# Buffers of five tags handed out by urgency, and two more prices in the plan of a hybrid decoder step

## The chip, the core and the metric

The kernel runs on one NeuronCore of a Trainium2 chip. The metric is the device time of one execution in microseconds (us), the median of several runs. Engines are named as the profile names them: PE is TensorE's matmul, PEld its weight load, DVE VectorE, ACT ScalarE, POOL GpSimd, SP SyncE, which issues most DMAs.

## What is computed

One inference step of a two-layer decoder trunk with width 1024, for a prompt of 2048 tokens and for a group of eight samples with one new token each and 2048 cached positions in pages of 128. Layer 0 joins a chunked spatial gate (A) and stick-breaking attention over eight heads (B); layer 1 joins sparse attention over the 256 best keys of an indexer (C) and causal pooling over windows of 2 to 16 (D). Everything is float32.

```python
hp, kvp, _ = even_mixer(xp, None, w_in_even[j], a_w_sp[j], a_b_sp[j])
past = gather_pages(cache_b_kv[j], page_table)
hs, kvs, vs = even_mixer(xs, past, w_in_even[j], a_w_sp[j], a_b_sp[j])
...
log_keep = jnp.where(mask, jax.nn.log_sigmoid(-z), 0.0)                    # B
later = lax.cumsum(log_keep, axis=3, reverse=True) - log_keep
att = jnp.where(mask, jnp.exp(jax.nn.log_sigmoid(z) + later), 0.0)
...
_, sel = lax.top_k(index, topk)                                            # C
logits = jnp.einsum('bqgrd,bqkgd->bqgrk', qg, k_sel) * HEAD_DIM ** -0.5
p = jax.nn.softmax(logits, axis=-1)
...
xp = post_norm(xp, hp, w_out[layer], ln_g[layer], ln_b[layer])
xs = post_norm(xs, hs, w_out[layer], ln_g[layer], ln_b[layer])
```

## The kernel before

The prompt is worked in four blocks of 512 tokens. A matmul that needs full accuracy is made of three: both operands are split into a high and a low part (`split`, line 640; `load_w`, line 656, for weights). `p0` is the input projection of layer 0, `p1a` and `p1b` are that of layer 1 (lines 735 to 737), `out_proj` is the output projection (lines 1132 to 1134), `mixer_b` is B (`z`, line 1027, then transposes `ps_p`, line 1064), `c_tile` is C (`z_c`, line 1763, read by DVE at line 1765; transposes `ps_pc`, line 1794), `index` and `topk` choose the keys (`z_i`, line 1453). At the end of `topk` DVE loads a flag (line 1594) and jumps over a rare exact search (line 1595); this happens 14 times. `sample0` and `sample1` do the eight samples; `sample1` fetches pages of the C cache with 64 indirect DMAs on POOL's queue (`rows`, line 2244), into two buffers.

`Body` emits all of it once, in a program order in which `par` mixes the streams by estimated costs. Then `Order` makes the order that the engines follow. `gather` collects dependences and, for each tag of tiles, the tiles in program order; `settle` prices every instruction, lets `plan` make 15 orders, replays each under two drawings of slightly changed prices (`replay`), and keeps the order with the least sum; `keep` writes it down as a fixed order for each engine. `plan` is a list scheduler: it starts, on each free engine, the ready instruction with the least rank, and the rank is the latest start that `latest` finds by scheduling backwards from the end.

A tag is a ring of buffers that tiles of one kind share. `plan` hands a tag's buffers out in program order: the next tile of a tag gets one only when the tile ahead of it has been begun. The tags that matter here are three pairs of PSUM banks, `pp` (projections), `pt` (transposes) and `pz` (the logits `z`, `z_c`, `z_i`, and the small `ps_s` and `ps_m`), and two SBUF tags with four buffers each, `tmp` and `ot`. `tmp` holds among others `lng` and `lnb`, the scales and shifts of the layer norm (`ln`, lines 1210 and 1211), in halves of 512 columns.

The plan's prices that the change touches: a DMA lands `DMA_START` (700 ns) + bytes over a rate + `DMA_END` (1500 ns) after its turn; a matmul that follows a pause costs `RESTART` (105 ns) more. The flag load is priced at 1300 ns and the jump at 400 ns.

Of the kernel before, what the change touches and what calls it, by code (L numbers as in the profile page):

```python
# [83 lines left out]


class Order:
# [55 lines left out]
    def gather(self):  # L142
# [174 lines left out]

    def settle(self):

        N, eng = len(self.ins), self.eng  # L320
        self.costs = [self.cost(n) for n in range(N)]
        for g, ms in self.group.items():
            busy = sum(self.costs[m][0] for m in ms)
            self.costs[g] = busy, busy + 170
        self.dma = [e is not None and "DMA" in i.opcode for e, i in zip(eng, self.ins)]
        self.kinds = [self.kind(n) for n in range(N)]
        self.ports = [self.port(n) for n in range(N)]
        self.succ = [[] for _ in range(N)]
        for n, d in enumerate(self.dep):
            for m in d:  # L330
                self.succ[m].append(n)
        self.links()
        draws, mid, best = [self.draw(k) for k in range(self.DRAWS)], self.costs, None
        sem = self.SEM
        for by, near in self.GUESSES:
            self.costs = [(b * by, l * by) if e in self.TAIL else (b, l) for e, (b, l) in zip(eng, mid)]
            self.SEM = near
            self.plan(list(range(N)))
            for _ in range(self.ROUNDS):
                self.SEM = near  # L340
                self.plan(self.latest())
                self.SEM = sem
                x = sum(self.replay(c) for c in draws)
                if best is None or x < best[0]:
                    best = x, self.order, self.after
        self.costs, (_, self.order, self.after) = mid, best

# [15 lines left out]
    def replay(self, cost):  # L363
# [9 lines left out]
        for n in range(N):  # L373
# [4 lines left out]
            left[n] = len(preds[n]) + (n in seq)  # L378
        start, done, idle, dma_end, count = [0.0] * N, [0.0] * N, [0.0] * N, 0.0, 0

# [14 lines left out]
        while ready:  # L395
            s, n = pop(ready)
            if self.ports[n]:
                asked.setdefault(n, s)
                if hold[self.OTHER[eng[n]]] > s:
                    push(ready, (hold[self.OTHER[eng[n]]], n))  # L400
                    continue
            count += 1
            if eng[n] is not None:
                busy, lat = cost[n]
                if self.ports[n]:
                    hold[eng[n]] = s + max(40, busy - self.RELEASE[eng[n]])
                if eng[n] == "PE" and n in seq and self.kinds[n] != self.kinds[seq[n]]:
                    s += 150 if "h" in (self.kinds[n], self.kinds[seq[n]]) else 0
                elif eng[n] == "PE" and n in seq and s > idle[seq[n]] + 1:
                    busy, lat = busy + self.RESTART, lat + self.RESTART  # L410
                start[n], idle[n], done[n] = s, s + busy, s + lat
                if self.dma[n]:
                    dma_end = max(s + self.DMA_START, dma_end) + lat
                    done[n] = dma_end + self.DMA_END
            else:
                start[n] = done[n] = idle[n] = s
            for m in succ[n]:
                left[m] -= 1
                if not left[m]:
                    push(ready, (when(m), m))  # L420
# [4 lines left out]
    def turns(self):  # L425
# [12 lines left out]
        return out  # L438

    def plan(self, rank):  # L440

# [9 lines left out]
        queue = {g: ts[::-1] for g, ts in self.tags.items()}  # L451
        free = {g: max(self.tiles[t].tag_meta.bufs for t in ts) for g, ts in self.tags.items()}
        open_ = dict.fromkeys(queue, True)
        users = {t: len(u) for t, u in self.uses.items()}
        self.after, gone = {}, {g: [] for g in queue}
        since, done, self.begun = [0.0] * N, [0.0] * N, [0.0] * N
# [26 lines left out]
        while count < N:  # L483
            while back and back[0][0] <= now:
                _, g, x = pop(back)
                free[g] += 1
                gone[g].append(x)
                take(g, now)
# [9 lines left out]
            for e, q in ready.items():  # L498
                while q and idle[e] <= now:
# [31 lines left out]
                    if self.dma[n]:  # L531
                        dma_end = max(s + self.DMA_START, dma_end) + lat
                        done[n] = dma_end + self.DMA_END
                    else:
# [7 lines left out]
                    for t in tiles[n]:  # L542
                        g, u = home[t], self.uses[t]
                        if n == u[0]:
                            open_[g] = True
                            for m in u[1:]:
# [12 lines left out]
    def latest(self):  # L559

        N, eng, push, pop = len(self.ins), self.eng, heapq.heappush, heapq.heappop
        cost = self.costs
        lat = [c[1] + self.SEM + (self.DMA_START + self.DMA_END if d else 0) for c, d in zip(cost, self.dma)]
        pred, left = [[] for _ in range(N)], [0] * N
# [48 lines left out]

    def keep(self):
        info = mybir.DependencyInfo(mybir.DependencyClass.NoSync, mybir.DependencyReason.DATA)
# [9 lines left out]
class Body:  # L625
    def __init__(self, ctx, tc, I, O):
        self.ctx, self.tc, self.nc, self.I, self.O = ctx, tc, tc.nc, I, O
        pool = lambda n, b, **k: ctx.enter_context(tc.tile_pool(name=n, bufs=b, **k))
        self.cst = pool("cst", 1)
# [37 lines left out]
    def rsqrt(self, out, var, eps, n):  # L667
# [9 lines left out]
        for _ in range(3):  # L677
# [3 lines left out]
            v.tensor_tensor(out, out, t[:n], op=OP.mult)  # L681

    def ps(self, name, shape=(P, TB)):

        b = next(b for b in BANKS.get(name, "pt").split() if b in self.banks)
        return self.banks[b].tile(list(shape), F32, tag=b, name=name)

    def tmp(self, name):
        return self.loc.tile([P, TB], F32, tag="tmp", name=name, bufs=self.bufs["tmp"])

# [396 lines left out]
    def otile(self, name):  # L1087
        return self.loc.tile([P, TB], F32, tag="ot", name=name, bufs=self.bufs["ot"])

# [1374 lines left out]

def build(nc, shapes):
    I = {n: nc.dram_tensor(n, s, d, kind="ExternalInput").ap() for n, s, d in shapes}
    O = {n: nc.dram_tensor("out_" + n, s, F32, kind="ExternalOutput").ap() for n, s in _OUTS}
    with tile.TileContext(nc, schedule_with_timeline_sim=True) as tc:
        with ExitStack() as ctx:
            body = Body(ctx, tc, I, O)  # L2470
            body.run()
        order = Order(tc, body.lags)
        order.gather()
        order.settle()
        order.keep()

# [12 lines left out]
```

## Time and profile before

| | |
|---|---|
| median of 3 runs | 2790.44 us (2785.44 to 2792.58) |
| the profiled execution | 2784.49 us |
| its span, first to last instruction | 2782.8 us |
| PE busy | 2672.8 us, 96% of the span |
| DVE, ACT, POOL busy | 2060.9, 1604.3, 766.3 us |
| mean granted clock of TensorE | 0.983 |

A busy share says how long an engine had an instruction in work, not that it worked at its best. Idle time of PE is listed with what ended it: the instruction of another engine, or the DMA, whose signal came last. The granted clock is 1.00 at 2.4 GHz and 0.50 at 1.2 GHz.

### The profile page before, as it was taken

To read this page: it belongs to the slowest core of one execution; us is meant where nothing else is said; L and a number is where in the kernel's file an instruction comes from. 1 tells how busy PE (TensorE), PEld (TensorE's weight loads), DVE (VectorE), ACT (ScalarE), POOL (GpSimd) and SP (SyncE) were. 2 spreads that over 40 slices of the span, in tenths; PEclk is the share of its full clock that TensorE was granted. 3 is DMA by queue.
4 is the path that set the end of the run, shared out by engine and by line. 5 is a ranking of instruction groups with operands and counts; after the bars stand their busy time and mean duration, and the time that the engine had idled before them with its cause. 6 is when DMAs were issued, how large, how long until landed. Compare 5 with 4: busy or idle time off the path is not lost. (4 is left out here: it accounts for less than half of the span.)

```text
span 2782.8 us, 52464 instructions
## 1 busy us (share of the span) xinstructions
PE 2672.8 (96%) x17490; PEld 2154.5 (77%) x17490; DVE 2060.9 (74%) x5557; ACT 1604.3 (58%) x3216; POOL 766.3 (28%) x1040
## 2 busy tenths in 40 slices
PE   9999999999999999989899999999999999899996
PEld 7888787777777887768677677778777889898985
DVE  3466568775857886747988888897898788888865
ACT  3434333444444354435657677786686788688854
POOL 0111112210202321033433522334411445344222
PEclk9999999999999999999999999999999999999998
DMA  8666857895777777563764545433675666767462
GB/s 251 168 186 207 266 169 245 242 302 161 224 213 205 222 207 249 181 178 116 211 199 132 166 131 157 127 102 115 190 220 149 199 192 200 221 200 235 125 197 81
DMA packets 538914, 524.58 MB, mean 189 GB/s; under 512 B 43447, under 2 KB 411224, under 8 KB 538607
## 3 DMA queue, kind: packets, MB, share of 16 engines
q1 hardware_dynamic: 528759, 485.34, 58.9%
q0 software_dynamic: 9856, 35.66, 4.1%
q8 instruction: 139, 2.28, 0.3%
q14 instruction: 160, 1.31, 0.1%
HBM read 431.33 MB, written 89.73 MB: 187 GB/s over the span
## 5 line engine op out<-in xcount | busy, mean ns | idle before, releaser
L735 PE MATMUL pp<-xh,wh 128*128 128x512 f32 (+1 forms) x1536 | 624.0, 408 | 2.5 <-ACT wh L661 1.6
L736 PE MATMUL pp<-xl,wh 128*128 128x512 f32 (+1 forms) x1536 | 615.4, 401 | 0.0
L737 PE MATMUL pp<-xh,wl 128*128 128x512 f32 (+1 forms) x1536 | 613.6, 400 | 0.0
L664 DVE TENSOR_TENSOR wl<-wr,wh 128x512 fp32r<-128x512 f32 x520 | 354.5, 699 | 161.7 <-ACT wh L661 146.8
L661 ACT CAST wh<-wr 128x1024 fp32r<-128x1024 f32 x260 | 270.2, 1040 | 321.4 <-PE pp L736 160.2
L735 PEld LDWEIGHTS pp<-xh,wh 128*128 128x128 f32 (+1 forms) x1536 | 287.6, 188 | 67.4 <-issue 8.5
L737 PEld LDWEIGHTS pp<-xh,wl 128*128 128x128 f32 (+1 forms) x1536 | 287.6, 187 | 61.5 <-issue 4.4
L736 PEld LDWEIGHTS pp<-xl,wh 128*128 128x128 f32 (+1 forms) x1536 | 288.2, 188 | 53.9 <-issue 5.3
L1132 PE MATMUL pp_o<-wh,oh 128*128 128x256 f32 x1008 | 294.2, 294 | 5.4 <-DVE xres L1137 3.6
L1133 PE MATMUL pp_o<-wl,oh 128*128 128x256 f32 x1008 | 290.5, 289 | 0.2 <-DVE wl L664 0.2
L1134 PE MATMUL pp_o<-wh,ol 128*128 128x256 f32 x1008 | 288.5, 289 | 0.0
L1065 ACT COPY P<-ps_p 128x512 f32<-128x512 f32 (+2 forms) x320 | 166.5, 524 | 178.3 <-PE ps_p L1064 156.2
L1041 DVE TENSOR_TENSOR_SCAN P<-P,bfst 128x512 f32<-128x512 f32 x192 | 250.0, 1317 | 14.5 <-ACT P L1034 7.6
L1763 PE MATMUL z_c<-ksc,qc 128*128 128x512 f32 (+3 forms) x816 | 221.3, 356 | 22.9 <-DVE mx L1765 13.1
L1781 ACT ACTIVATE zt<-zt,nmax 128x512 f32<-128x512 f32 (+3 forms) x320 | 209.6, 657 | 54.1 <-DVE nmax L1769 52.2
L1750 POOL TENSOR_TENSOR nm<-nm,mk 128x256 f32<-128x256 f32 (+1 forms) x128 | 98.4, 770 | 420.2 <-DMA nm<-bft 161.3
L1796 ACT COPY zt<-ps_pc 128x512 f32<-128x512 f32 (+3 forms) x320 | 163.8, 522 | 81.6 <-PE ps_pc L1794 79.2
L1027 PE MATMUL z<-ks,q 128*128 128x512 f32 (+3 forms) x640 | 195.0, 390 | 13.1 <-DVE mx L1765 5.1
L1132 PEld LDWEIGHTS pp_o<-wh,oh 128*128 128x128 f32 x1008 | 193.3, 192 | 12.6 <-DVE xres L1137 4.6
L1133 PEld LDWEIGHTS pp_o<-wl,oh 128*128 128x128 f32 x1008 | 194.3, 193 | 4.1 <-issue 1.1
L1134 PEld LDWEIGHTS pp_o<-wh,ol 128*128 128x128 f32 x1008 | 193.4, 193 | 4.5 <-issue 2.2
L1509 ACT ACTIVATE mk<-ix,tk_tn 128x1152 int8<-128x1152 f32 (+13 forms) x140 | 183.8, 1313 | 17.7 <-DVE tk_tn L1559 6.6
(455 smaller groups left out, 5518.0 us busy)
## 6 DMA issues: line engine op xcount, KB each, us to landing
pg<-cache_b_kv SPq DMA_DIRECT2D x256, 256.0 KB
wr<-w_in_even SPq DMA_DIRECT2D x112, 512.0 KB
wr<-w_in_odd SPq DMA_DIRECT2D x76, 512.0 KB
wr<-w_out SPq DMA_DIRECT2D x68, 512.0 KB
ks<-ksc SPq DMA_DIRECT2D x80, 256.0 KB
ksc<-kcs SPq DMA_DIRECT2D x80, 256.0 KB
q<-qsc SPq DMA_DIRECT2D x64, 256.0 KB
qc<-qcs SPq DMA_DIRECT2D x128, 128.0 KB
```

The source lines that it names most:

```text
L661: nc.scalar.copy(hi, raw)
L664: e.tensor_tensor(lo[:, c], raw[:, c], hi[:, c].bitcast(F32), op=OP.subtract)
L735: nc.tensor.matmul(ps[:m], wh[:, kt, :m], xh[kt], start=a, stop=False)
L736: nc.tensor.matmul(ps[:m], wh[:, kt, :m], xl[kt], start=False, stop=False)
L737: nc.tensor.matmul(ps[:m], wl[:, kt, :m], xh[kt], start=False, stop=b)
L1027: nc.tensor.matmul(z[:, :n], q2[:, c, t * P:(t + 1) * P].bitcast(F32R), ks[:, :n].bitcast(F32R), start=c == 0, stop=c == 1)
L1041: nc.vector.tensor_tensor_scan(r, r, r, initial=ini, op0=OP.mult, op1=OP.bypass)
L1132: nc.tensor.matmul(ps[:, :256], oh[:, tt], wh[:, k], start=a, stop=False)
L1133: nc.tensor.matmul(ps[:, :256], oh[:, tt], wl[:, k], start=False, stop=False)
L1134: nc.tensor.matmul(ps[:, :256], ol[:, tt], wh[:, k], start=False, stop=b)
L1763: nc.tensor.matmul(z[:, :n], q2[:, c, jj % 2, :].bitcast(F32R), kk, start=c == 0, stop=c == 1)
L1781: nc.scalar.activation(zt, zt, AF.Exp, bias=nmx, accum_out=st["rs"][:, h, c:c + 1])
```

## The change

Two things change in `Order`. First, for five tags (`ot`, `tmp`, `pt`, `pz`, `pp`) `plan` no longer hands buffers out in program order alone. When a buffer is free, `choose` looks at the eight tiles of the tag with the least rank; it takes the first of them for which a free buffer exists whose last tile stands earlier in the program, and for which `safe` finds that all tiles passed over can still be placed. To make the buffer binding, the kernel is built twice: the first build plans and stops with the exception `Planned`; the second gives every tile of these tags the buffer of the plan, as a tag of its own with one buffer (`turn`), and follows the planned order. Of the other tags the plan now notes a buffer as well, but doesn't bind it.

Second, prices: a DMA on POOL's queue (all page gathers) lands 2500 ns later in the plan (`GATHER`), in `plan`, `replay` and `latest`; and in `replay`, by which the 15 orders are compared, a PE instruction that starts over 1300 ns after the one before it (`PAUSE`) opens 4500 ns (`WARM`) in which PE's instructions cost up to twice their time. `plan` itself doesn't know this second price. No instruction of the computation is added or removed.

```diff
+FREELY = ('ot', 'tmp', 'pt', 'pz', 'pp')
...
+    GATHER = 2500
+    PAUSE, WARM = 1300, 4500
+    AHEAD, WINDOW = 10**6, 8
...
+        last = lambda n: max(self.group.get(n, (n,)))
+        self.span = {t: (u[0], max(map(last, u))) for t, u in self.uses.items()}
+        self.free = {g for g, ts in self.tags.items() if g.split("_")[0] in FREELY}
...
+        self.ends = [self.DMA_END + (self.GATHER if e == "POOL" else 0) for e in eng]
...
+                if eng[n] == "PE" and n in seq:
+                    cold = s + self.WARM if s > idle[seq[n]] + self.PAUSE else cold
+                    if s < cold:
+                        busy, lat = busy + min(busy, cold - s), lat + min(busy, cold - s)
...
-                    done[n] = dma_end + self.DMA_END
+                    done[n] = dma_end + self.ends[n]
...
+    def safe(self, queue, held, x, b):
+
+        held = [(f, self.span[t][1] if t else -1) for f, t in held]
+        if x:
+            held[b] = self.span[x]
+        far = max(f for f, _ in held)
+        for t in queue:
+            if t == x:
+                continue
+            first, end = self.span[t]
+            if first > far:
+                return True
+            fit = [(f, k) for k, (f, e) in enumerate(held) if f < first and e < first]
+            if not fit:
+                return False
+            held[max(fit)[1]] = first, end
+        return True
+
+    def choose(self, queue, urgent, free, held, pending, any_):
+
+        least = queue[0]
+        if pending and (not any_ or self.span[pending][0] < self.span[least][0]):
+            return None
+        for x in urgent[:self.WINDOW] if any_ and not pending else ():
+            first = self.span[x][0]
+            if x != least and first > self.span[least][0] + self.AHEAD:
+                continue
+            for _, b in sorted(((held[b][0], b) for b in free if held[b][0] < first), reverse=True):
+                if self.safe(queue, held, x, b):
+                    return x, b
...
-            while queue[g] and free[g] and open_[g]:
-                x = queue[g].pop()
-                if gone[g]:
-                    self.after[x] = gone[g].pop(0)
-                free[g] -= 1
-                open_[g] = False
+            while queue[g] and free[g]:
+                x = self.choose(queue[g], urgent[g], free[g], held[g], open_[g], g in self.free)
+                if x is None:
+                    return
+                x, b = x
...
+    def turn(self, pool, shape, tag, name, **k):
+
+        if tag not in self.made:
+            return pool.tile(shape, F32, tag=tag, name=name, **k)
+        if self.slots:
+            k, tag = {"bufs": 1}, f"{tag}{self.slots[tag][len(self.made[tag])]}"
+        t = pool.tile(shape, F32, tag=tag, name=name, **k)
+        self.made[tag.rstrip("0123456789")].append(t.tensor.name)
+        return t
...
+    try:
+        build(bacc.Bacc("TRN2", target_bir_lowering=False, num_devices=1), shapes)
+    except Planned as x:
+        build(nc, shapes, x.args)
```

## Rows read from the trace of the kernel before

**Rows 1.** The page's head and its part 1: busy time of each engine, share of the span, and instructions.

```profile
span 2782.8 us, 52464 instructions
PE 2672.8 (96%) x17490; PEld 2154.5 (77%) x17490; DVE 2060.9 (74%) x5557; ACT 1604.3 (58%) x3216; POOL 766.3 (28%) x1040
```

**Rows 2.** The view by stretches, over the whole span: start and end, length, then busy time of each engine with its instructions, the granted clock of TensorE, the busy share of the DMA engines and GB/s. The last stretch begins where the last matmul ends.

```profile
0.00:1235.00 1235.00, 1218.04 (x6818) 954.06 (x6819) 808.53 (x1483) 523.01 (x966) 210.22 (x332) 1.00 0.71 215
1235.00:2000.00 765.00, 721.98 (x4788) 560.62 (x4787) 632.40 (x1998) 511.01 (x1125) 281.74 (x415) 0.98 0.54 151
2000.00:2400.00 400.00, 386.92 (x2855) 328.98 (x2854) 336.63 (x1144) 303.72 (x593) 144.78 (x162) 0.99 0.65 195
2400.00:2600.00 200.00, 190.98 (x1622) 174.79 (x1622) 163.88 (x560) 156.60 (x306) 80.12 (x88) 0.96 0.65 202
2600.00:2757.50 157.50, 154.85 (x1418) 136.10 (x1414) 106.65 (x342) 106.93 (x226) 39.77 (x38) 1.00 0.42 132
2757.50:2782.80 25.30, 0.00 (x0) 0.00 (x0) 12.81 (x34) 3.04 (x4) 9.63 (x8) 0.60 0.51 167
```

**Rows 3.** The view of groups by line for PE: line, operation, out<-in, shapes, count, busy us, mean ns of one, then idle time of PE just before them and what ended it.

```profile
L1132 PE MATMUL pp_o<-wh,oh 128*128 128x256 f32 x1008 | 294.2, 294 | 5.4 <-DVE xres L1137 3.6 <-ACT oh L648 0.9 <-DVE fq L1586 0.6
...
L1763 PE MATMUL z_c<-ksc,qc 128*128 128x512 f32 (+3 forms) x816 | 221.3, 356 | 22.9 <-DVE mx L1765 13.1 <-ACT r L1456 2.7 <-DVE s_rq L2124 2.0
L1027 PE MATMUL z<-ks,q 128*128 128x512 f32 (+3 forms) x640 | 195.0, 390 | 13.1 <-DVE mx L1765 5.1 <-DMA ks<-ksc 4.4 <-ACT P L1031 2.2
L1794 PE MATMUL ps_pc<-idf,zt 128*128 128x128 f32 x1088 | 182.0, 279 | 2.0 <-ACT zt L1796 0.7 <-ACT P L1065 0.7 <-ACT s16o L1148 0.4
L1064 PE MATMUL ps_p<-idf,P 128*128 128x128 f32 x1088 | 180.7, 276 | 5.8 <-ACT P L1065 4.6 <-DVE hT L762 1.0
...
L1453 PE MATMUL z_i<-kid,qi 128*128 128x512 f32 (+3 forms) x160 | 63.8, 417 | 7.8 <-DMA qi<-qis 5.4 <-ACT r L1456 1.4 <-DVE mx L1765 0.9
```

**Rows 4.** DVE's first instruction after one of the 14 jumps, in order of time: start us, us, what; in brackets the idle time before it and what ended it.

```profile
1557.80 1.01 DVE L1511 TENSOR_SCALAR_CACHE_REDUCE mk<-ix,tk_tn 128x768 int8<-128x768 f32 x1 [3.63 <-DVEq L1595]
```

**Rows 5.** The view of waits for DVE, two of the nine lines that end on the jump's sequencer: who waited, for what, us in total, times, longest; and the jump's own line.

```profile
DVE mk L1511 <- DVEq L1595: 10.8, 3, 4.1
...
DVE ri L1822 <- DVEq L1595: 0.9, 1, 0.9
```

```profile
L1595 DVEq COMPARE_BRANCH  x14: 56/72/76, 1419.1 to 2643.9; - x14
```

**Rows 6.** PE in order of time: the first, the longest and the last of nine pauses (0.60 to 5.11 us, 20.5 us together) that begin while DVE stands at a jump, or within 6 us after it.

```profile
1495.87 0.58 PE L1763 MATMUL z_c<-ksc,qc 128*128 128x256 f32 x2 [2.05 <-DVE mx L1765]
```

```profile
1562.49 1.01 PE L1027 MATMUL z<-ks,q 128*128 128x384 f32 x2 [5.11 <-DVE mx L1765]
```

```profile
2651.73 0.72 PE L1763 MATMUL z_c<-ksc,qc 128*128 128x512 f32 x2 [1.22 <-DVE mx L1765]
```

**Rows 7.** The view by stretches, over the stretches inside the work in which the granted clock was 0.50, columns as in rows 2: four after jumps, then three after gathers, then two after other waits for PSUM, then three in other places, and their sum.

```profile
1496.20:1499.50 3.30, 3.30 (x10) 2.60 (x9) 3.30 (x9) 1.08 (x3) 1.83 (x2) 0.50 1.06 267
1561.10:1567.80 6.70, 5.31 (x26) 4.57 (x27) 4.47 (x20) 1.69 (x5) 1.96 (x3) 0.50 0.09 23
1643.00:1646.30 3.30, 3.30 (x9) 2.30 (x8) 2.60 (x10) 2.02 (x6) 1.24 (x3) 0.50 0.28 60
2120.80:2124.20 3.40, 3.40 (x11) 2.52 (x10) 3.37 (x10) 3.22 (x4) 0.75 (x2) 0.50 0.00 0
2486.10:2489.40 3.30, 3.30 (x16) 3.11 (x14) 2.83 (x4) 3.30 (x6) 0.67 (x1) 0.50 0.94 311
2516.80:2523.50 6.70, 6.59 (x33) 5.09 (x31) 4.85 (x12) 4.45 (x12) 5.38 (x5) 0.50 0.79 254
2533.90:2540.60 6.70, 6.70 (x30) 5.55 (x30) 3.82 (x18) 3.31 (x9) 1.89 (x4) 0.50 1.00 298
1984.30:1991.00 6.70, 5.91 (x27) 5.07 (x29) 4.12 (x24) 5.07 (x13) 1.93 (x2) 0.50 1.06 305
2390.50:2397.20 6.70, 5.99 (x26) 5.79 (x27) 4.82 (x14) 2.31 (x7) 0.25 (x1) 0.50 0.48 161
...
sum 73.80, PE 63.88 PEld 52.71 DVE 50.18 ACT 36.27 POOL 25.62; mean PE 5.32 PEld 4.39 DVE 4.18 ACT 3.02 POOL 2.13
```

**Rows 8.** Gathers: PE's waits for them (view of waits), one gather on POOL and the matmul that it kept waiting (order of time), and the first and last matmul that reads the gathered values, and the sample's first in the output projection that follows (views of lines 2304 and 1145; duration ns least/median/most, first and last start).

```profile
PE ps_so L2304 <- DMA s_pg<-cache_c_kv,s_rq: 7.0, 4, 2.4
...
PE ps_so L2304 <- DVE mx L1765: 1.8, 1, 1.8
```

```profile
2478.28 0.97 POOL L2244 DMA_INDIRECT s_pg<-cache_c_kv,s_rq  x1 [0.15 <-PE ps_rb L1828]
```

```profile
2483.82 0.92 PE L2304 MATMUL ps_so<-s_lg,s_pg 128*128 128x8 f32 x7 [1.39 <-DMA s_pg<-cache_c_kv,s_rq]
```

```profile
L2304 PE MATMUL ps_so<-s_lg,s_pg x256: 170/256/361, 2402.5 to 2613.2; 128*128 128x8 f32 x128
```

```profile
L1145 PE MATMUL ps_so<-wh,osx x32: 276/276/361, 2662.2 to 2732.1; 128*16 128x256 f32 x32
```

**Rows 9.** The end, in order of time: the last load of a scale on SP's queue, ACT's layer norm of the last rows, and POOL's multiplication that needs both.

```profile
2768.05 0.69 SPq L1210 DMA_DIRECT2D lng<-ln_g  x1
...
2768.70 1.52 ACT L1214 ACTIVATE xres<-xres,ln_nb,ln_rs 128x512 f32<-128x512 f32 x2 [3.72 <-DVE ln_nb L1205]
...
2772.91 1.26 POOL L1215 TENSOR_TENSOR xres<-xres,lng 128x512 f32<-128x512 f32 x1 [5.03 <-DMA lng<-ln_g]
```

More of the change, by code (lines that the diff above doesn't have):

```diff
@@ L316, in port, with settle @@
                 and all(map(sb, (*full, i.outs[0]))))
-    def settle(self):
+    def settle(self, plan):
         N, eng = len(self.ins), self.eng
@@ L332, in settle @@
         self.links()
+        if plan:
+            self.order, self.after = plan[:2]
+            return
         draws, mid, best = [self.draw(k) for k in range(self.DRAWS)], self.costs, None
@@ L344, in settle @@
                 if best is None or x < best[0]:
-                    best = x, self.order, self.after
-        self.costs, (_, self.order, self.after) = mid, best
+                    best = x, self.order, self.after, self.slot
+        self.costs, (_, self.order, self.after, self.slot) = mid, best
     def draw(self, seed):
@@ L438, in turns @@
         return out
+    def safe(self, queue, held, x, b):
[25 more added lines that the diff above has]
+                    return x, b
+        fit = sorted(((held[b][0], b) for b in free if held[b][0] < self.span[least][0]), reverse=True)
+        for _, b in fit:
+            if self.safe(queue, held, least, b):
+                return least, b
+        return (least, fit[0][1]) if fit and not any_ else None
     def plan(self, rank):
@@ L450, in plan @@
                     tiles[n].append(t)
-        queue = {g: ts[::-1] for g, ts in self.tags.items()}
-        free = {g: max(self.tiles[t].tag_meta.bufs for t in ts) for g, ts in self.tags.items()}
-        open_ = dict.fromkeys(queue, True)
+        queue = {g: list(ts) for g, ts in self.tags.items()}
+        urgent = {g: sorted(ts, key=lambda t: (rank[self.uses[t][0]], t)) if g in self.free else queue[g]
+                  for g, ts in self.tags.items()}
+        bufs = {g: max(self.tiles[t].tag_meta.bufs for t in ts) for g, ts in self.tags.items()}
+        free = {g: list(range(k)) for g, k in bufs.items()}
+        held = {g: [(-1, None)] * k for g, k in bufs.items()}
+        open_ = dict.fromkeys(queue)
         users = {t: len(u) for t, u in self.uses.items()}
-        self.after, gone = {}, {g: [] for g in queue}
+        self.after, self.slot = {}, {}
         since, done, self.begun = [0.0] * N, [0.0] * N, [0.0] * N
@@ L468, in take @@
         def take(g, t):
-            while queue[g] and free[g] and open_[g]:
-                x = queue[g].pop()
-                if gone[g]:
-                    self.after[x] = gone[g].pop(0)
-                free[g] -= 1
-                open_[g] = False
+            while queue[g] and free[g]:
+                x = self.choose(queue[g], urgent[g], free[g], held[g], open_[g], g in self.free)
+                if x is None:
+                    return
+                x, b = x
+                queue[g].remove(x)
+                if urgent[g] is not queue[g]:
+                    urgent[g].remove(x)
+                free[g].remove(b)
+                self.slot[x] = b
+                if held[g][b][1]:
+                    self.after[x] = held[g][b][1]
+                held[g][b] = self.span[x][0], x
+                open_[g] = x
                 for n in self.uses[x]:
@@ L485, in plan @@
                 _, g, x = pop(back)
-                free[g] += 1
-                gone[g].append(x)
+                free[g].append(self.slot[x])
                 take(g, now)
@@ L532, in plan @@
                         dma_end = max(s + self.DMA_START, dma_end) + lat
-                        done[n] = dma_end + self.DMA_END
+                        done[n] = dma_end + self.ends[n]
                     else:
@@ L562, in latest @@
         cost = self.costs
-        lat = [c[1] + self.SEM + (self.DMA_START + self.DMA_END if d else 0) for c, d in zip(cost, self.dma)]
+        lat = [c[1] + self.SEM + (self.DMA_START + x if d else 0) for c, d, x in zip(cost, self.dma, self.ends)]
         pred, left = [[] for _ in range(N)], [0] * N
@@ L612, in latest, with keep @@
         return [-s - c[0] for s, c in zip(start, cost)]
-    def keep(self):
+    def keep(self, plan):
+        if not plan:
+            raise Planned(self.order, self.after, {g: [self.slot.get(t, 0) for t in ts] for g, ts in self.made.items()})
         info = mybir.DependencyInfo(mybir.DependencyClass.NoSync, mybir.DependencyReason.DATA)
@@ L1087, in otile @@
     def otile(self, name):
-        return self.loc.tile([P, TB], F32, tag="ot", name=name, bufs=self.bufs["ot"])
+        return self.turn(self.loc, [P, TB], "ot", name, bufs=self.bufs["ot"])
     def out_parts(self, i, layer, last):
@@ L2469, in build @@
         with ExitStack() as ctx:
-            body = Body(ctx, tc, I, O)
+            body = Body(ctx, tc, I, O, plan and plan[2])
             body.run()
@@ L2473, in build @@
         order.gather()
-        order.settle()
-        order.keep()
+        order.made = body.made
+        order.settle(plan)
+        order.keep(plan)
 def kernel(**inputs):
```

17 lines of the change are left out of this document (10 added, 7 removed).

## The prediction

> **What bounds the kernel now.** I read the page's part 1 first. PE is busy 2672.8 of 2782.8 us [rows 1], so a better order can win only from the 110.0 us in which PE has nothing in work, and from stretches at the lower clock. The view by stretches says where the 110 lie: 17.0 up to 1235 us, 43.0 up to 2000, 13.1 up to 2400, 9.0 up to 2600, 2.7 up to the last matmul, and 25.3 behind it [rows 2] (length less PE's busy time, each). The first 1235 us are nearly full, the rest of the change is decided in the second half. The view of groups by line says for what PE waits there: six lines have 57.0 us of idle time before them, and except for 10.7 us of loads and operands (qi 5.4, ks 4.4, oh 0.9) it ends on a reader of PSUM, that is, on a bank of `pz`, `pt` or `pp` that comes free [rows 3]. So 46.3 us are waits for exactly the rings that the change sets free. The clock is the other part: inside the work it stood at 0.50 for 73.8 us in twelve stretches, with 63.88 us of PE work in them [rows 7]; at 1.2 instead of 2.4 GHz half of that, 31.9 us, is lost.
>
> **Waits that the plan doesn't see.** Before the 46.3 us are given to the change, I look at what is behind them. DVE jumps 14 times [rows 5]. At the one near 1553 us it stood idle 3.63 us for the jump's sequencer [rows 4]; over all, fourteen such waits in nine lines make 41.5 us, up to 4.1 each [rows 5]. Nine pauses of PE, 20.5 us in all, begin at such a place, with 2.05, 5.11 and 1.22 us for the first, the longest and the last [rows 6]: PE stands at `z_c` or `z` because DVE hasn't read the bank. The plan prices the jump at 0.4 us and goes on pricing it so; an order cannot avoid what it doesn't know. I leave these 20.5 us, and the clock lost behind them (four stretches, 15.31 us of PE work, half of it 7.7) [rows 7], as they are. The Trainium skill (Advanced Engine Details and Errata, Control Flow Timing) gives a compare-and-branch some 108 ns; the trace disagrees, 3.63 us of idle time. By that figure the 20.5 us would be common ring waits and half of them and of their 7.7 us would go too, some 14 us more.
>
> **Term 1, the rings.** 46.3 - 20.5 = 25.8 us of ring waits remain. The tiles of `pz` and `pt` are filled and read within one step of the program, so no two of them overlap there, and `safe` has no reason to refuse: any of the eight most urgent may go first. Tiles of `pp` live over many steps, two of `out_proj` at a time, so little changes there. Where a `z_c` waits because DVE is behind, a `z` or `z_i`, whose reader is ACT, can now take the bank; from 1235 to 2000 us DVE is busy 83% and ACT 67% of the time (632.40 and 511.01 of 765) [rows 2], so there is room on ACT. But where both are late nothing helps. Ends: 0 and -25.8; no row decides, I take half, **-12.9**. Two stretches at 0.50 (5.91 and 5.99 us of PE work) stand behind such waits [rows 7]; they cost 6.0, and I take the same half, **-3.0**.
>
> **Term 2, the gathers.** The plan's old prices (0.7 + 1.5 us, 512 KB over its rate, 0.2 for a signal) make a gather some 4.4 us. In the trace one issued at 2478.28 kept PE waiting until 2483.82, which is 5.5 us [rows 8]. With 2.5 us more the plan allows 6.9, so it no longer puts the matmul too early. PE waited 7.0 us for gathers and once 1.8 us at the same line, put down to DVE [rows 8], and three stretches at 0.50 stand behind (16.59 us of PE work, 8.3 lost) [rows 7]: 17.1 in all. Ends 0 and -17.1; since 6.9 covers the 5.5 with room, I take the greater part, **-12**. The Trainium skill (DMA: Bandwidth & Descriptors, Anatomy of one DMA) fits such a DMA as 2.0 us + bytes / 436e3, here 3.2 us as an estimate; the trace disagrees with 5.5. That is a rival below.
>
> What does the longer gather cost? The 32 gathers of values are used over 2402.5 to 2613.2 us, one in 6.6; with two buffers 6.9 us of gather and some 1 us of use allow one in 4.0. And the chain ends 49 us before the sample's projection starts at 2662.2 [rows 8]. So I cost it at nothing; without that cover, 32 x 2.5 / 2 = 40 us of chain would appear. On POOL's queue the gathers (0.97 us each) move ahead of splits and masks; POOL is busy 80.12 of 200 us there [rows 2], which hides them.
>
> **Term 3, the end.** Behind the last matmul there are 25.3 us [rows 2]. `lng` and `lnb` are tiles of `tmp`, handed out in program order, so the last rows' scale is loaded after the sample's, at 2768.05. ACT's first half is ready some 0.8 us after 2768.70, but POOL starts at 2772.91, after 5.03 us of idle time that ended on that load [rows 9]. With `tmp` free, the load the end hangs on may go first. Ends 0 and -5.0 (no gain beyond POOL's idle time); I take **-4**; late next are POOL's and DVE's own steps.
>
> **Small or unknown.** The charge for pauses acts only through which of the 15 orders is kept; it can gain no more than clock that is already in terms 1 and 2: 0. A bound buffer is an added wait: a tile must now wait for its own bank even if the other comes free first, and on PE everything queued behind it waits too. No row shows such a case; the plan prices it itself, so I take 0, with +12.9 (it eats term 1) and 0 as ends. Loads into `ot` and `tmp` come earlier on SP; the DMA engines are busy 0.42 to 0.71 there [rows 2].
>
> **Sum.** -12.9 - 3.0 - 12 - 4 = -31.9 us. The profiled execution took 2784.49 us, 6.0 less than the median 2790.44. So 2784.5 - 31.9 = 2752.6, and on the scale of the median 2758 us, -1.2%. The forecast's own range: with terms 1 to 3 full (-25.8, -6.0, -17.1, -5.0) 2736, with a third of the sum 2780.
>
> **Rivals.** (a) *The next late thing.* The rings are not short of places but of readers: whichever tile takes the bank, DVE or ACT reads it as late, and PE's pause moves to the next tile. For it: DVE is busy 84% from 2000 to 2400 us [rows 2], and 20.5 of 46.3 us were DVE's in any case. Against it: ACT has room, and the waits for gathers have nothing to do with rings. If term 1 is nothing and what PE gains at gathers is lost at the next bank, the end's 4 us remain: 2786 us, no change that a measurement here could tell (about 0.3%, 8.4 us).
>
> (b) *The jumps get dearer.* A plan that fills PE and DVE tighter leaves less work between a tile and its reader, and a jump it prices at 0.4 us then shows on PE in full. Place: the 14 jumps. Price: if each stops PE for 4.1 us, the longest hold [rows 5], that is 57.4 us against 20.5 now, +36.9; with one stretch of 3.35 us at 0.50 behind each (as after three of the four [rows 7]), 23.5 us lost against 7.7, +15.8. With the gains of the sum, +52.7 - 31.9 = +20.8: 2811 us. It decides from a mean pause of 3.1 us per jump (now 1.5), where the gains are eaten, and makes it measurably slower from 3.5. For it: the 5.11 us at 1562.49 [rows 6]. Against it: five jumps show no pause at PE today, and tighter does not mean tighter at these places.
>
> (c) *The gather was priced well enough.* If a gather as a rule lands within the old 4.4 us and the four waits are exceptions of a busy DMA path (0.65 there [rows 2]), term 2 is nothing: 2770 us. This is what the 3.2 us of the Trainium skill (DMA: Bandwidth & Descriptors) would mean.
>
> That the change doesn't do what it says would be `safe` refusing nearly all; then (a) holds.
>
> **How the numbers follow.** Forecast 0.58, (a) 0.16, (b) 0.18, (c) 0.08. Faster by over 0.3% (under 2782) are the forecast and (c), 0.66; (a) is within, 0.16; (b) slower, 0.18. The range reaches down beyond the full terms by some of the jumps' 28 us, to 2728, and up into (b), where part of its price is paid and a bound buffer costs something, to 2806.
>
> **What would show it.** Right: idle time before lines 1763, 1027, 1453, 1794, 1064 and 1132 falls from 57 to some 44 us; PE's waits on the gathered pages fall from 7.0 to under 2; fewer stretches at 0.50 between 2400 and 2600 us; the tail behind the last matmul 21 instead of 25.3 us; PE's busy time a little under 2672.8. Wrong: idle time at the jumps well over 20 us (b); the same idle time under other readers' names (a); gathers that wait as before. The forecast fails altogether if PE's order now starves a stream whose weights or loads come late, which would show as waits for `wh` or loads before line 735.

## The result, and the profile after

The median went from 2789.86 us (2785.44 to 2792.58, four runs) to 2752.57 us (2751.04 to 2771.42, four runs): a ratio of 0.9883, with a 95% interval of 0.9838 to 0.9928 (the ratios here are those of the means, so they differ a little from those of the medians). The profiled execution after took 2754.03 us, 30.5 less than the profiled one before. The page's head and part 1 of the changed kernel, to be held against [rows 1]:

```profile
span 2752.2 us, 52410 instructions
...
PE 2660.1 (97%) x17490; PEld 2148.5 (78%) x17490; DVE 2048.3 (74%) x5557; ACT 1600.4 (58%) x3216; POOL 775.3 (28%) x1040
```

PE runs the same 17490 instructions. The span is 30.6 us shorter, 12.7 of it in PE's busy time and 17.9 in its idle time. The view by stretches, columns as in [rows 2], with the borders moved so that each stretch ends at about the same point of the work:

```profile
0.00:1222.00 1222.00, 1208.62 (x6768) 946.10 (x6769) 800.39 (x1477) 516.51 (x955) 203.27 (x327) 1.00 0.72 215
1222.00:1977.00 755.00, 723.63 (x4862) 566.44 (x4860) 638.12 (x2022) 515.49 (x1138) 295.73 (x422) 0.99 0.56 157
1977.00:2372.00 395.00, 381.48 (x2796) 325.24 (x2796) 324.78 (x1116) 297.96 (x580) 146.22 (x160) 0.97 0.65 195
2372.00:2570.00 198.00, 193.71 (x1675) 175.29 (x1673) 169.91 (x580) 161.90 (x320) 79.23 (x88) 0.99 0.65 204
2570.00:2728.00 158.00, 152.65 (x1398) 135.41 (x1396) 101.15 (x332) 105.50 (x223) 41.79 (x39) 0.99 0.43 134
2728.00:2752.20 24.20, 0.00 (x0) 0.00 (x0) 13.94 (x34) 3.04 (x4) 9.12 (x8) 0.57 0.52 175
```

Length less PE's busy time gives the idle time of each: 13.4, 31.4, 13.5, 4.3, 5.3 and 24.2 us, against 17.0, 43.0, 13.1, 9.0, 2.7 and 25.3. Most of what was won lies in the second stretch, where layer 1's first tiles run beside layer 0's last, and in the fourth, that of the gathers. The last is nearly as long as it was.

The view of groups by line for PE answers to [rows 3] (lines 1132, 1763, 1027, 1794, 1064 and 1453 are now 1213, 1844, 1108, 1875, 1145 and 1534); the seventh row is the matmul behind the gathers of values:

```profile
L1213 PE MATMUL pp_o<-wh,oh 128*128 128x256 f32 x1008 | 293.6, 294 | 6.7 <-ACT oh L719 3.9 <-DVE xres L1218 2.6
L1844 PE MATMUL z_c<-ksc,qc 128*128 128x512 f32 (+3 forms) x816 | 220.8, 354 | 20.4 <-DVE mx L1846 14.3 <-DMA ksc<-kcs 2.9 <-DVE fq L1666 1.3
L1108 PE MATMUL z<-ks,q 128*128 128x512 f32 (+3 forms) x640 | 189.9, 381 | 7.5 <-DMA ks<-ksc 3.2 <-DVE mx L1846 2.8 <-ACT P L1112 1.1
L1875 PE MATMUL ps_pc<-idf,zt 128*128 128x128 f32 x1088 | 181.2, 278 | 4.1 <-ACT zt L1862 3.3 <-DVE xl L725 0.5
L1145 PE MATMUL ps_p<-idf,P 128*128 128x128 f32 x1088 | 180.7, 276 | 3.9 <-DVE hT L843 2.2 <-DVE P L1122 0.9 <-ACT P L1146 0.5
L1534 PE MATMUL z_i<-kid,qi 128*128 128x512 f32 (+3 forms) x160 | 62.9, 406 | 1.0 <-ACT r L1537 0.6 <-DVE mx L1846 0.2
...
L2385 PE MATMUL ps_so<-s_lg,s_pg 128*128 128x8 f32 x256 | 32.0, 242 | 1.6 <-DVE s_acc L2390 1.6
```

The six lines have 43.6 us of idle time, where 57.0 stood. Loads and operands have 14.8 of it (oh 3.9, `zt` 3.3 that ACT had not finished, ks 3.2, ksc 2.9, `P` 0.9, qc 0.6). Counted the same way they had 12.0 before, the prediction's 10.7 with 1.1 of ksc and 0.2 of `zt`, which stand behind the three releasers that [rows 3] shows. So the waits for a bank fell from 45.0 to 28.8. The gathered pages no longer appear among what PE waits for: 7.0 us became nothing, and with the wait put down to DVE the line went from 8.8 to 1.6. The prediction's other sign for them held too: between the first and the last matmul that reads gathered values there were three stretches at 0.50, now there is one.

The stretches inside the work at a granted clock of 0.50 (1.2 GHz), answering to [rows 7]; there are again twelve of them, but shorter ones, and their sum is:

```profile
sum 49.90, PE 48.03 PEld 42.30 DVE 30.22 ACT 28.15 POOL 25.77; mean PE 4.00 PEld 3.52 DVE 2.52 ACT 2.35 POOL 2.15
```

PE's work in them fell from 63.88 to 48.03 us; half of the difference, 7.9 us, is what the clock gave back (in the trace of before, one transpose of line 1794 followed another after 109 ns in the median at 1.00 and after 213 at 0.50). It is most of the 12.7 us by which PE is less busy.

What stayed are the pauses at DVE's jumps. One of them in order of time, first on DVE (two rows of one timeline), then on PE, as in [rows 4] and [rows 6]:

```profile
1612.87 0.17 DVE L1623 TENSOR_SCALAR tk_okn<-tk_tn 128x5 f32<-128x5 f32 x1
1617.08 0.16 DVE L1624 TENSOR_TENSOR tk_oh<-tk_okn 128x4 f32<-128x4 f32 x1 [4.04 <-DVEq L1676]
```

```profile
1614.60 0.40 PE L816 MATMUL pp<-xh,wh 128*128 128x512 f32 x1
1617.91 0.74 PE L1844 MATMUL z_c<-ksc,qc 128*128 128x512 f32 x2 [2.92 <-DVE mx L1846]
```

DVE stands 4.04 us at the jump. PE has projection work for the first half, then the next thing in its fixed order is a `z_c` whose bank DVE hasn't read, and it stands 2.92 us. Sixteen pauses that begin while DVE stands at a jump or within 6 us after it make 22.1 us (20.5 in nine before). 17.4 us of them are waits for a bank before the six lines, three fifths of the 28.8 us that are left there.

The end, from the timeline of POOL and that of SP's queue; it answers to [rows 9]:

```profile
2742.94 2.48 POOL L1296 TENSOR_TENSOR xres<-xres,lng 128x512 f32<-128x512 f32 x2 [5.26 <-DMA lng<-ln_g]
```

```profile
2737.05 1.37 SPq L1291 DMA_DIRECT2D lng<-ln_g  x2
```

POOL again waits over 5 us for the same kind of load, which again is issued late.

### The profile page after: what moved, and what is told of

The parts are those of the page before. It is cut to its first block, busy times and chain, and to the rows that moved or that the text cites. A ratio compares the mean times of both kernels' runs of the same rounds, so it can differ in the third digit from the quotient of the medians.

```text
span 2752.2 us, 52410 instructions
## 1 busy us (share of the span) xinstructions
PE 2660.1 (97%) x17490; PEld 2148.5 (78%) x17490; DVE 2048.3 (74%) x5557; ACT 1600.4 (58%) x3216; POOL 775.3 (28%) x1040
## 5 line engine op out<-in xcount | busy, mean ns | idle before, releaser
L1844 PE MATMUL z_c<-ksc,qc 128*128 128x512 f32 (+3 forms) x816 | 220.8, 354 | 20.4 <-DVE mx L1846 14.3
L1590 ACT ACTIVATE mk<-ix,tk_tn 128x512 int8<-128x512 f32 (+13 forms) x140 | 183.5, 1311 | 19.9 <-DVE tk_tn L1640 7.4
```

Of the source, the lines that this page charges most:

```text
L1844: nc.tensor.matmul(z[:, :n], q2[:, c, jj % 2, :].bitcast(F32R), kk, start=c == 0, stop=c == 1)
```

## The experiments

All twelve kernels are timed against the kernel before on the same chip, so each ratio has its own runs of before beside it (its median there: 2779.77 us with the first four, 2779.14 with the next four, 2778.75 with the last four). e6 and e10 are variants of the kernel before, the others of the changed one. The numbers first:

| kernel | median us | ratio to before, 95% |
|---|---|---|
| e1 in program order, all prices | 2808.04 | 1.0100 (1.0071 to 1.0130) |
| e2 freedom for PSUM tags only | 2768.19 | 0.9959 (0.9944 to 0.9975) |
| e3 freedom for SBUF tags only | 2767.41 | 0.9951 (0.9934 to 0.9969) |
| e4 freedom, no gather price | 2749.10 | 0.9896 (0.9866 to 0.9926) |
| e5 binding alone | 2778.52 | 1.0003 (0.9986 to 1.0019) |
| e6 before, with the gather price | 2807.49 | 1.0103 (1.0083 to 1.0123) |
| e7 after, second family of orders | 2752.74 | 0.9908 (0.9886 to 0.9931) |
| e8 after, own tiles at the end | 2778.84 | 1.0000 (0.9987 to 1.0012) |
| e9 after, no charge for pauses | 2749.13 | 0.9884 (0.9865 to 0.9902) |
| e10 before, second family of orders | 2815.86 | 1.0132 (1.0109 to 1.0155) |
| e11 after, third family of orders | 2752.24 | 0.9905 (0.9885 to 0.9925) |
| e12 after, jump priced at 3600 ns | 2724.94 | 0.9807 (0.9787 to 0.9826) |

**Which part gives the gain.** Four kernels, each the changed one with a part taken back.

```diff
-    AHEAD, WINDOW = 10**6, 8
+    AHEAD, WINDOW = 10**6, 0                   # e1
...
-FREELY = ('ot', 'tmp', 'pt', 'pz', 'pp')
+FREELY = ('pt', 'pz', 'pp')                    # e2
+FREELY = ('ot', 'tmp')                         # e3
...
-    GATHER = 2500
+    GATHER = 0                                 # e4
```

> Buffers of the five tags in program order again (the window of urgent tiles is empty); both new prices and the binding of buffers stay. Theory (the freedom empties the waits for PSUM banks, the gather's price the waits for pages): about half of the gain goes, 2765 to 2775 us, idle time of PE before the six lines that fill PSUM back at some 55 us, no waits for gathered pages. Rival A (the prices alone do it): 2750 to 2757 us. Rival B (only all together): 2785 to 2795 us.

> Only the three PSUM tags are free and bound; tmp and ot go in program order as before. Theory (the freedom that counts is that of the PSUM banks): within 5 us of the changed kernel, 2750 to 2758 us. Rival (earlier loads and results in tmp and ot bring it): 2765 to 2785 us.

> Only tmp and ot are free and bound; the PSUM banks go in program order as before. Theory: as without any freedom, 2765 to 2775 us, waits for PSUM banks as before the change. Rival (tmp and ot bring it): 2750 to 2758 us.

> A gather is priced as before the change, the rest is as changed. Theory: PE waits again 5 to 9 us for gathered pages and two or three stretches at 0.50 stand behind them, 2762 to 2770 us. Rival (the old price was good enough, the waits were exceptions): 2750 to 2756 us, no such waits.

Without freedom (e1) the gain is not only gone, the kernel is 1% slower than before: 94.2 us idle inside the work against 84.7 [rows 2], and 31.0 us of pauses at the jumps. With all freedom and no gather price (e4) it is all there. Either kind of tag alone (e2, e3) gives less than half of it against the kernel before, but about two thirds against e1 (1.4 and 1.5 of 2.1%), and the two orders are of different families (below). The groups by line show where the two differ, e2 first:

```profile
L1844 PE MATMUL z_c<-ksc,qc 128*128 128x512 f32 (+3 forms) x816 | 219.8, 353 | 17.2 <-DVE mx L1846 9.2 <-ACT P L1112 2.1 <-issue 1.8
```

```profile
L1844 PE MATMUL z_c<-ksc,qc 128*128 128x512 f32 (+3 forms) x816 | 222.3, 355 | 29.2 <-DVE mx L1846 18.9 <-DMA ksc<-kcs 6.3 <-ACT P L1112 2.2
```

With PSUM free, `z_c` waits less; with SBUF alone free it waits more than before [rows 3], and still e3 is as fast as e2. So the waits for banks that the freedom of PSUM spares are not the whole story, and I had said nothing of what `ot` and `tmp` do inside the work. With one order each, how the gain is shared between the two kinds is not shown.

In e4 PE waits for gathers again (the view of waits):

```profile
PE ps_so L2385 <- DMA s_pg<-cache_c_kv,s_rq: 3.5, 5, 1.6
```

The whole kernel shows no cost of this: 0.9896 against the changed kernel's 0.9884 in e9. But the time is a sum of two differences. From the first to the last matmul that reads gathered values, nearly the same number of matmuls takes longer without the price; the view by stretches, columns as in [rows 2], for the changed kernel, for e9 (the same order once more, below) and for e4, then e4's longest stretch at 0.50, which begins 6 us after a wait of 1.56 us for a gather:

```profile
2378.60:2609.90 231.30, 226.64 (x1998) 204.24 (x1997) 197.38 (x685) 192.91 (x385) 96.06 (x105) 0.99 0.64 199
```

```profile
2373.30:2607.40 234.10, 228.78 (x1998) 205.68 (x1997) 198.04 (x683) 193.01 (x386) 94.98 (x105) 0.99 0.64 197
```

```profile
2362.00:2603.60 241.60, 235.75 (x2008) 212.46 (x2007) 197.73 (x681) 191.54 (x383) 96.18 (x105) 0.95 0.61 189
```

```profile
2483.30:2500.30 17.00, 17.00 (x88) 13.70 (x87) 9.80 (x39) 9.88 (x22) 6.79 (x10) 0.50 0.88 297
```

PE's idle time and half of its work at 0.50 make 17.5 us there in e4, as in the kernel before, against 6.4 in the changed kernel and 8.7 in e9. What e4 lost there it had won earlier: it reaches the first of these matmuls 11 us before e9. Its order parts from the changed kernel's at 1650 us, so whether the price or the draw of an order did that is open.

**Binding, the gather price alone, and a second order of the same rules.** e5 is the changed kernel without freedom and without both prices; e6 adds only the gather price to the kernel before; e7 lets the planner choose among five of its fifteen orders only, those of the second of its three starting guesses.

```diff
-    GATHER = 2500
-    PAUSE, WARM = 1300, 4500
-    AHEAD, WINDOW = 10**6, 8
+    GATHER = 0                                 # e5
+    PAUSE, WARM = 10**9, 4500
+    AHEAD, WINDOW = 10**6, 0
...
-                    done[n] = dma_end + self.DMA_END
+                    done[n] = dma_end + self.ends[n]    # e6, on the kernel before
...
-    GUESSES = ((1.0, 200), (1.0, 250), (1.04, 230))
+    GUESSES = ((1.0, 250),)                    # e7
```

> Buffers in program order, old prices (no longer gather, no pause), only the binding of buffers of the five tags and the double build remain. Theory A (the prices without freedom made the run with buffers in program order slow): as the kernel before, 2772 to 2788 us on this chip. Theory B (binding a tile to one buffer costs that): 2798 to 2812 us, more waits for PSUM banks than before the change.

> The kernel before with one edit: a DMA on POOL's queue lands 2500 ns later in the plan. Theory A (the gather's price without freedom made the run with buffers in program order slow): 2795 to 2812 us. Theory B (binding did): 2765 to 2780 us, 7 us of waits for gathered pages gone.

> The changed kernel, but only five of the 15 orders are compared, so that another order made by the same rules is kept. Theory (the freedom brings the gain, whichever order is kept): within 10 us of the changed kernel, 2745 to 2763 us. Rival (the gain is the luck of one order): anywhere from 2745 to 2800 us, over 2763 more likely than not.

Binding shows no cost: 1.0003. (It is not a pure test: e5's order is not that of before, PE's orders part after 693 of the 17490 matmuls.) e5 and e1 differ in the prices alone and by 1%, and e6 is as slow as e1, so it looked as if the gather price made an in-order plan worse. But the line that it is meant for does not bear that out. The groups by line of e5, then of e1:

```profile
L2385 PE MATMUL ps_so<-s_lg,s_pg 128*128 128x8 f32 x256 | 32.4, 248 | 4.8 <-DMA s_pg<-cache_c_kv,s_rq 3.1 <-DVE mk L1592 0.9 <-DVE c_sum L1913 0.5
```

```profile
L2385 PE MATMUL ps_so<-s_lg,s_pg 128*128 128x8 f32 x256 | 32.0, 242 | 0.0
```

With the price PE's wait at the gathers is gone, as it should be, and the kernel is slower by 1% elsewhere. What else changes with a price is which order is kept, and e6 kept one of the second family, made from the second guess. That called for the kernel before with an order of that family and no new price. The traces tell the families apart: the orders of PE in before, e1, e3, e4, e5, e8, e9 and e12 begin with the same 628 matmuls as that of the changed kernel; those of e2, e6, e7 and e10 leave that order after 37 and share their own first 612.

**Is it the prices or the draw of an order?** e10 is the kernel before with the second guess alone, e11 the changed kernel with the third alone, e9 the changed kernel without the charge for pauses.

```diff
-    GUESSES = ((1.0, 200), (1.0, 250), (1.04, 230))
+    GUESSES = ((1.0, 250),)                    # e10, on the kernel before
+    GUESSES = ((1.04, 230),)                   # e11
...
-    PAUSE, WARM = 1300, 4500
+    PAUSE, WARM = 10**9, 4500                  # e9
```

> The changed kernel without the price of pauses. Of the 15 orders the same one is kept, so that the program is instruction for instruction the changed one: 0.983 to 0.993 of the kernel before on every theory. It stands here as the changed kernel on the chip of the three runs beside it.

> The kernel before, with only five of its 15 orders compared, so that another order is kept; nothing else. Theory (freedom brings the gain, and orders scatter around it): within 1% of the kernel before, 2765 to 2810 us, and over every free order but the one with tiles of its own at the end. Rival (an order is luck, free or not): as low as 2750 us is as likely as 2790.

> The changed kernel, with the last five of its 15 orders compared (VectorE, ScalarE and GpSimd priced 4% dearer while the order is made), so that a third order is kept. Theory: 2745 to 2768 us, under every order with buffers in program order. Rival (luck): half the time over 2770 us.

Without the charge for pauses the planner keeps the same order (PE's 17490 matmuls and DVE's 5557 instructions come in the same order in both traces), so e9 is the changed kernel measured once more: 0.9884. e10 has no new price and is the slowest of all. The same pause stands in e10 and in e6 (the view of waits for PE of each):

```profile
PE pp_o L1134 <- POOL ol L654: 9.0, 3, 3.8
```

```profile
PE pp_o L1135 <- POOL ol L655: 9.9, 3, 3.8
```

In the trace of before PE has no wait of this kind. So e6 need not be slow by the price: an order of its family is as slow without it. For e1 that reason falls away, since its order is of the first family, like those of before and e5.

Put together: with buffers in program order the planner's rules gave 1, 1.0003, 1.0100, 1.0103 and 1.0132; with all five tags free 0.9884, 0.9896, 0.9905, 0.9908 and 1.0000 (e8, below). The means are 1.0068 and 0.9919. The groups touch at one point only, and inside each the times scatter by over 1%, several times the interval of any single ratio. Not all in a group share the same prices; e9 and e8, with two orders of one family, are 1.2% apart.

**The end.** e8 gives three of the four `lng` and `lnb` tiles of the last rows buffers of their own, so that their loads hang on no ring.

```diff
-        self.late = self.ln_late([self.xlast], dst[3 * P:TB], None, 1)
+        self.late = self.ln_late([self.xlast], dst[3 * P:TB], None, 1, True)
...
-            g, b = self.tmp("lng"), self.tmp("lnb")
+            g, b = (self.tw.tile([P, TB], F32, tag=f"{x}{c}", name=x, bufs=1) if own and (x, c) != ("lnb", 1)
+                    else self.tmp(x) for x in ("lng", "lnb"))
```

> The changed kernel, but three of the four scale and shift tiles of the last rows' layer norm have buffers of their own instead of tmp, so that their loads can be made early. Theory (the end waits for a load that has no free buffer): the stretch behind the last matmul falls from 24 to some 19 us, 2745 to 2750 us. Rival (the load's place in SP's queue or DVE's chain holds the end): the stretch stays at 23 to 25 us, 2750 to 2756 us.

The tail stayed at 24.3 us (24.2 in the changed kernel). The timeline of POOL, then that of DVE, shows the next late thing:

```profile
2770.63 1.26 POOL L1297 TENSOR_TENSOR xres<-xres,lng 128x512 f32<-128x512 f32 x1 [3.89 <-ACT xres L1296]
```

```profile
2768.76 0.68 DVE L1298 TENSOR_TENSOR xs_ln<-xs_ln,lnb 8x512 f32<-8x512 f32 x1 [2.99 <-DMA lnb<-ln_b]
2769.37 0.14 DVE L752 TENSOR_TENSOR ln_rs<-ln_rs,rs_t 128x1 f32<-128x1 f32 x1
2769.55 0.16 DVE L1286 SCALAR_TENSOR_TENSOR ln_nb<-ln_mv,ln_rs 128x1 f32<-128x1 f32 x1
```

POOL no longer waits for the load; it waits for ACT, and ACT for `ln_nb`, a few tenths of a microsecond of DVE's work that stands in its queue behind the samples' step, which waits 2.99 us for a load of the samples' own `lnb`. The whole kernel is no faster than before, though, and that is not the tail: PE's order parts from the changed kernel's at 1943 us, and from 2200 us on the work runs otherwise. The waits of PE:

```profile
PE z_c L1845 <- DVE mx L1847: 26.4, 22, 4.7
```

Against 14.3 us in the changed kernel, with 34.3 us of pauses at jumps against 22.1. A change of 24 us of work at the end has given the planner another order, and that order happens to put its `z_c` at the jumps.

**The jumps.** If the pauses at the jumps stay because the plan prices a jump at 0.4 us, a plan that is told 3.6 us, near what DVE was seen to stand [rows 4], should be able to go round them.

```diff
-            return (400, 400) if type(i).__name__ == "BassTileConditionalBlock" else (30 if e else 0, 30)
+            return (3600, 3600) if type(i).__name__ == "BassTileConditionalBlock" else (30 if e else 0, 30)
```

> The changed kernel, with the jump over the exact search priced at 3.6 us on VectorE instead of 0.4. Theory (PE stands at the jumps because the plan doesn't know their length): PE's pauses at the jumps fall from 22 us to under 12, time 2738 to 2748 us. Rival (the plan has nothing to put there, the wait only moves): pauses as before, 2748 to 2765 us.

This is the fastest of all, 2724.94 us, 0.9807 of before and 0.9912 of the changed kernel beside it (2749.13 in e9). Page, head and part 1:

```profile
span 2721.2 us, 52412 instructions
...
PE 2650.4 (97%) x17490; PEld 2144.3 (79%) x17490; DVE 2040.0 (75%) x5557; ACT 1598.1 (59%) x3216; POOL 770.5 (28%) x1040
```

DVE still stands as long at the jumps. The view of line 1676 in e12, duration ns least/median/most, first and last start us; the second row is the next instruction of that line on DVE's sequencer:

```profile
L1676 DVEq COMPARE_BRANCH  x14: 67/70/72, 1409.3 to 2586.3; - x14
L1676 DVEq EVENT_SEMAPHORE  x14: 21/21/21, 1413.2 to 2589.9; - x14
```

From the end of the one to the start of the other it is 2.8 to 4.9 us, 51.6 over the 14, against 51.4 in the changed kernel and 47.3 before. One of them on DVE, and PE in the meantime:

```profile
1672.71 1.28 DVE L1592 TENSOR_SCALAR_CACHE_REDUCE mk<-ix,tk_tn 128x1024 int8<-128x1024 f32 x1 [4.58 <-DVEq L1676]
```

```profile
1668.17 0.39 PE L817 MATMUL pp<-xl,wh 128*128 128x512 f32 x1
...
1669.32 0.82 PE L1875 MATMUL ps_pc<-idf,zt 128*128 128x128 f32 x6
...
1671.83 0.40 PE L818 MATMUL pp<-xh,wl 128*128 128x512 f32 x1
1672.06 0.22 PE L834 MATMUL ps_smp<-wh,xsT 128*16 128x128 f32 x1
...
1673.01 0.60 PE L1145 MATMUL ps_p<-idf,P 128*128 128x128 f32 x4
```

For 4.58 us PE is given projections and transposes, nothing that DVE must read first, and does not stand. PE's waits for `z_c`'s reader (the view of waits) fall from 14.3 us to:

```profile
PE z_c L1844 <- DVE mx L1846: 3.9, 8, 1.9
```

Pauses at jumps fell from 22.1 us in sixteen to 2.7 in two, idle time inside the work from 67.9 to 46.9 us. The difference of the two, 21.0 us, is about the size of the pauses (19.4). e12 too is one order and one draw. It lies below all the other free orders, by more than four of those five differ among themselves, and the row that was to change did. But fewer pauses at the jumps are not a gain by themselves: e11, which is told nothing of them, has 11.1 us in ten and only 8.6 us of waits for `z_c`'s reader, and is no faster than e9. That the price of the jump is worth 0.9% under other orders too is not shown.

## Why the prediction came out as it did

The forecast of 2758 us lies 5 us above the median, and its sum of -31.9 us beside the -30.6 of the two profiled spans. In the rows of the two traces terms 1 and 2 came out close to their size, term 3 did not. That the total came out so close is luck in part: another order of the same rules (e8, with one small edit at the end) has no gain.

**The basis** held: PE's idle time inside the work and the stretches at 0.50 gave 16.8 + 7.9 of the 30.6 us, the tail 1.1, and 4.8 us are PE's busy time that the clock does not account for. The 46.3 us of bank waits were 1.3 too many: 1.1 of a load (ksc) and 0.2 of an operand (`zt`).

**Term 1, the rings** (-12.9 and -3.0). The row came out as named, 57 to 43.6 us. Without the share of the jumps the bank waits fell from 24.5 us (45.0 - 20.5) to 11.4 (28.8 - 17.4), which is -13.1; up to the first matmul on gathered values the clock gave back 2.9. That it was the freedom rests on the two groups of orders (means 1.0068 and 0.9919), not on this one pair. I had given the gain to the PSUM tags; e3 shows as much for `ot` and `tmp` alone, by a way that I have not traced.

**Term 2, the gathers** (-12). In its place the term came out: the line's waits went from 8.8 to 1.6 us, and idle time with half the work at 0.50 from 17.5 to 6.4 in the section of the gathers, -11.1. With the price out both are largely back there (e4: 3.5 us of waits, 17.5 in the section). As a gain of the whole kernel it is not shown: e4 is as fast, by an order that is ahead before the gathers begin. The interval of the difference of the two ratios, some 10 us either way, and the scatter of orders are as large as the term. That the longer gather costs nothing is not shown apart from this either. Rival (c) named a total of 2770 us, which was not reached, and its reason fell: in the changed kernel a gather lands 4.4 to 9.5 us after its issue, 5.1 in the median of 64, so the old 4.4 us was the least and not the rule (the view of DMAs, with the median):

```profile
s_pg<-cache_c_kv,s_rq POOLq DMA_INDIRECT x64, 5.1
```

**Term 3, the end** (-4) failed: -1.1. The load may go first now, but the plan did not let it. e8 shows what stands behind it: I named DVE's own steps as next late, but not that one of them stands behind another load.

**The jumps** were left as they were, and that held: 20.5 us became 22.1. e12 supports the reason given, that the order could not avoid what it didn't know: told, it avoids 19.4 of 22.1 us. As a rule it is too strong, since e11 has half of them untold.

**Small terms.** The charge for pauses at 0 held exactly (e9, same order kept). The bound buffer at 0 is borne out by e5 as far as another order can tell.

**The rivals.** (a), no freedom worth having because the readers are late, fell: the idle time of PE fell by 16.8 us and did not come back under other names. (b), jumps dearer by 37 us, fell for this order; e8's 34.3 us at the jumps show its mechanism at less than half that size, and e8 has no gain left. That an order's draw can move the time by 1% either way, with all prices the same, was in none of my cases; the chance that I gave to slower was right to be there, but for another reason.

**Open.** Why e1 is 1% slower than e5: both orders are of the first family (PE's first 1479 matmuls are the same), so either the two prices or the draw within a family did it, and e1's own order was not tried without its prices. What freedom in `ot` and `tmp` gives inside the work. And how wide the scatter of orders is: five in program order and five free ones are few.

## What to carry to other kernels

A planner sets out to hide only the stalls that it is charged for; others it misses by luck. Look in the trace for an engine that stands where the plan thinks it runs, and price that (here one number, and the one order made with it was 0.9% faster). A wait that vanishes from a trace is not a gain of the whole until the time without that edit is measured, and with a planner nearly every edit draws a new order as well: judge by several orders on either side, since here two orders of the same rules lay up to 1.3% apart. When a term is smaller than that scatter, compare its own section of the two traces, by the same count of matmuls; the total can't tell.

## What the hardware showed that I had not expected

A jump over a skipped block (no instruction of the block is in the traces) leaves DVE idle for microseconds: 41.5 us over 14 jumps before, up to 4.1 each [rows 5], 1.6 to 4.2 each after, and still 2.5 to 4.6 in the eleven that e12's waits list, where nearly nothing on PE waits for it any more. The jump's own instruction takes 56 to 76 ns [rows 5]. The Trainium skill (Advanced Engine Details and Errata, Control Flow Timing) gives some 108 ns for a compare-and-branch. That is more than the instruction took here, and far less than the stop behind it.

The clock goes with the pauses. Stretches at 0.50 and PE's idle time inside the work, kernel by kernel: 19 and 98.4 us in e10, 17 and 95.6 in e6, 18 and 94.2 in e1, 15 and 86.1 in e8, 12 and 84.7 before, 13 and 81.1 in e5, 8 and 76.4 in e2, 14 and 76.3 in e3, 12 and 67.9 after, 10 and 67.8 in e9, 8 and 64.2 in e4, 6 and 63.5 in e7, 12 and 61.3 in e11, 7 and 46.9 in e12. The order is roughly the same in both, with exceptions such as e2 and e11. So what an order saves in pauses it saves a second time, in part and not always, by the clock.
